# One fused decoder block: x ahead of c in the first stage, Silu of c behind the squares of x

## The chip, the cores and the metric

The kernel runs on one core of one Trainium2 chip. The metric is device time in microseconds of one execution of the whole program; lower is better. The core has five engines with a queue each: PE (TensorE, with its weight loads shown apart as PEld), DVE (VectorE), ACT (ScalarE), POOL (GpSimd) and SP (SyncE, which here only issues DMAs). A queue is worked off in order; an instruction that waits for another engine or for a DMA holds those behind it.

## The reference, cut to what matters

One sequence of 512 tokens, width 1024, one layer, all in float32.

```python
cs  = silu(c)                                   # c: (1, 1024)
mod = cs @ ada_w + ada_b                        # 1024 x 6144
sh_m, sc_m, gt_m, sh_f, sc_f, gt_f = split(mod, 6)
h = rmsnorm(x, norm_mix_g) * (1 + sc_m) + sh_m
q, k, v, g_ret, b_cv, c_cv, u_cv, g_a, g_b = split(h @ w_in)
q, k = rope(q, cos, sin), rope(k, cos, sin) * d**-0.5   # cos, sin of positions * inv_freq
y_a = (silu(g_ret) * head_layernorm(retention(q, k, v))) @ ret_w_out
y_b = (b_cv * causal_conv3(c_cv * u_cv)) @ conv_w_out
x = x + gt_m * ((sigmoid(g_a) * y_a + sigmoid(g_b) * y_b) @ mix_w_out)
# then a SwiGLU feed-forward part with sh_f, sc_f, gt_f, and a last rmsnorm
```

## The kernel before, in words

Features lie on the partitions in tiles of 128 (8 k tiles), tokens along the free axis (512). Every product is made of three matmuls on a high and a low part of each operand, so each weight tile is first cast by ACT (`_h`) and then subtracted by DVE (`_l`).

**First stage (L132 to L436).** SP loads c, then x in four tiles of 512 KB (`x_load`, L333), then the first pair of k tiles of the modulation weights as eight pieces of 256 KB (`ada_load`), then the first weights of c, u, b and k (`w_load`). POOL makes the constants `eps_t`, `ident` and `ones32` and issues the small loads: the rows of ada_b, the two norm gains and conv_w (L150 to L153), positions (`posi`, L155) and inv_freq (`ivf`, L157). ACT takes Silu of c into `cs` (L162) and runs one Sqrt on a constant (`warm`, L165). From L347 on every engine is in strict order, so the code from L398 to L576 is the order of each queue. For each x tile t: `x_squares(t)` (ACT: Square with a sum, then Sqrt), `x_scaled(t)` (DVE: reciprocal and scaling; PE: eight transposes), `x_by_feature(t, h)` (copies out of PSUM on ACT or DVE). `busy(n)` is n matmuls on constants that fill PE's time. `quarters()` makes three small constants from `ident` on DVE (L239). `mod_row` multiplies pieces of ada_w with `cs` on PE into two banks; `ada_sum` adds four other pieces weighted by `cs` on DVE into `acc_m`; `mod_sums` brings these sums into the same banks on PE. The two banks give the gains of the first two k tiles (`a_m`, `s_m`), ACT makes the modulated `Hh` of a k tile with them, and the first products `p_c`, `p_u`, `p_b`, `p_k` start.

**Pairs of k tiles (L545 to L576).** For j = 2, 4, 6 the next pair of modulation weights and of weights is loaded, if there is one, and the products of the pair before run.

**After that (from L577) the order is not written out.** Instructions are given to a scheduler that lays out each engine's queue ahead of time from its own estimate of when operands are ready; what it may estimate, the chip may not find. In this part lie the rotary angles on DVE (`rotary`, L298 and L597 to L601, from `posi` and `ivf` into `fr`), the value projection `p_v`, the tables `ropeC` and `ropeS` (`rope_tables`, L640: eight Sin activations on ACT), `rope` of a k or q tile (L651: four products and a sum on DVE, then a split), and the retention of a head pair. For the first pair the projections come in the order k (heads 0, 1), q (0, 1), gate (0, 1). `scores(u)` (L730) is due some projections later, set by `after(2 + u, ...)`; the first scores tile `st` is three matmuls of the rotated q and k of head 0.

Sin, Silu and Sqrt are activation functions that need a table to be loaded in ACT: an ACT_TABLE_LOAD stands in ACT's queue wherever the next function is not in the table loaded last; Copy, Identity and Square need none of their own.

`tc.issue_after(i)` puts what is issued inside it behind instruction i, on the engine of i.

Of the kernel before, what the change touches and what calls it, by code (L numbers as in the profile page):

```python
# [15 lines left out]
AF = mybir.ActivationFunctionType  # L16
# [3 lines left out]
P = 128  # L20
# [50 lines left out]
def block_kernel(ctx, tc, x, c, positions, ada_w, ada_b, norm_mix_g, w_in, conv_w, ret_w_out,  # L71
# [3 lines left out]
    pe, vec, act, pool, sync = (InTurn(tc, e) for e in (nc.tensor, nc.vector, nc.scalar, nc.gpsimd,  # L75
                                                        nc.sync))
# [13 lines left out]
    def scr(name, dt=F32, shape=None):  # L90
        return tp.tile(shape or [P, S], dt, tag="scr", bufs=12, name=name)
# [4 lines left out]
    def acc(name):  # L96
        return ps.tile([P, S], F32, tag="acc", bufs=4, name=name)
# [33 lines left out]

    HS = S // 2  # L132
    c_sb = cp.tile([P, KT], F32, name="c_sb")
    sync.dma_start(c_sb, c.rearrange("o (p k) -> (o p) k", p=P))
    rows = cp.tile([P, P], F32, name="rows")
    vec.memset(rows, 0.0)
    R_ADA, R_GM, R_GF, R_CW = 0, 48, 56, 64
# [2 lines left out]
    eps_t = cp.tile([P, 1], F32, name="eps_t")  # L140
# [8 lines left out]
    with tc.issue_after(pool.last.ins):  # L149
        small.dma_start(rows[0:48], ada_b.rearrange("o (r p) -> (o r) p", p=P))  # L150
        small.dma_start(rows[48:56], norm_mix_g.rearrange("o (r p) -> (o r) p", p=P))
        small.dma_start(rows[56:64], norm_ffn_g.rearrange("o (r p) -> (o r) p", p=P))
        small.dma_start(rows[64:88], conv_w.rearrange("o t (r p) -> (o t r) p", p=P))  # L153
        for i in range(2):
            small.dma_start(posi[64 * i:64 * i + 64],  # L155
                            positions[0, HS * i:HS * (i + 1)].partition_broadcast(64))
        small.dma_start(ivf, inv_freq.rearrange("(f o) -> f o", o=1))  # L157
# [1 line left out]
    x2 = x[0].rearrange("(t p) (h n) -> t h p n", p=P, n=S)  # L159

    cs = cp.tile([P, KT], F32, name="cs")
    act.activation(cs, c_sb, AF.Silu)  # L162
    warm = cp.tile([P, 1], F32, name="warm")
    with tc.issue_after(act.last.ins):
        act.activation(warm, eps_t, AF.Sqrt)  # L165

    onesr = cp.tile([P, P], F32R, name="onesr")

# [2 lines left out]
    def rows_by_feature(tr):  # L171
        vecs.append(cp.tile([P, P], F32, name="vecs"))
        act.copy(vecs[0], tr[:, 0:P])
# [24 lines left out]
    def ada_load(f, j):  # L198


        s0 = 0 if f == "m" else 3
        cols = slice(j * P, (j + 2) * P)
        ada_raw[f, j] = pieces = []
        for k in range(0, KT, 4):
            raw = wp.tile([P, 4, 2, 2 * P], F32, tag="raw", bufs=3, name=f"ada_{f}{j}_{k}")
            for q, i in ((q, i) for q in range(0, 4, 2) for i in range(2)):
                load_raw.last = sync.dma_start(raw[:, q:q + 2, i],
                                               aw6[:, k + q:k + q + 2, s0 + i, cols])
            pieces += [raw[:, q].rearrange("p s n -> p (s n)") for q in range(4)]
# [16 lines left out]
    def mod_gains(f):  # L226

        r0 = R_ADA + ADA["sc_" + f] // P
        g0 = R_GM if f == "m" else R_GF
        vec.scalar_tensor_tensor(mod["b_" + f], vecs[0][:, r0:r0 + KT], 1.0, vecs[0][:, g0:g0 + KT],  # L230
                                 ALU.add, ALU.mult)
# [7 lines left out]
    def quarters():  # L239
        quart["sum"] = cp.tile([P, 4, QP], F32, name="quart_sum")  # L240
        cols = sp.tile([P, QP], F32, tag="quart", bufs=1, name="quart_cols")
        vec.tensor_reduce(cols, ident.rearrange("p (q c) -> p c q", q=4), axis=AX.X, op=ALU.add)
        vec.tensor_copy(quart["sum"], cols.unsqueeze(1).to_broadcast([P, 4, QP]))
        quart["own"] = cp.tile([P, 4], F32, name="quart_own")
        vec.tensor_reduce(quart["own"], ident.rearrange("p (q c) -> p q c", q=4), axis=AX.X,
                          op=ALU.add)
        quart["f"] = cp.tile([P, 2 * D // QP], F32, name="quart_f")
# [85 lines left out]
    def x_load():  # L333
        for t in range(NT):
            xt = wp.tile([P, 2, S], F32, tag="hi", name=f"x_{t}")
            xs[t] = [xt[:, h] for h in range(2)] + [xt.rearrange("p h n -> p (h n)")]
            load_raw.last = sync.dma_start(xs[t][2], x[0, t * P:(t + 1) * P, :])

    def w_load(k):
        for n in "cubk":  # L340
            cols = P if n == "k" else 2 * P
            w_raw[n, k] = scr(f"w_{n}0_{k}", F32, [P, 2, cols])
            load_raw.last = sync.dma_start(
                w_raw[n, k], wi[k * P:(k + 2) * P, COL[n]:COL[n] + cols].rearrange(
                    "(k p) n -> p k n", p=P))
# [5 lines left out]
    def busy(n):  # L351

        for _ in range(n):
            mm(idle[:, 0:P], lhsT=ident, rhs=ident, start=True, stop=True)
# [8 lines left out]
    def x_squares(t):  # L363
        junk = scr(f"n1_{t}", BF16, [P, D])
        act.activation(junk, xs[t][2], AF.Square, accum_out=ssq[:, t:t + 1])
        act.activation(r4[:, t:t + 1], ssq[:, t:t + 1], AF.Sqrt, scale=1.0 / D, bias=eps_t)

    def x_scaled(t):
        r = r4[:, t:t + 1]
        vec.reciprocal(r, r)  # L370
        vec.tensor_scalar_mul(xs[t][2], xs[t][2], r)
        for h in range(2):
            txs[t, h] = acc(f"tx_{t}{h}").rearrange("p (k n) -> p k n", n=P)
            for k in range(4):
                transpose(txs[t, h][:, k], xs[t][h][:, k * P:(k + 1) * P], ident)
# [7 lines left out]
    def mod_row(j, k, banks, first, cols=range(4)):  # L383


        for i in cols:
            mm(banks[i % 2][:, i * P:(i + 1) * P], lhsT=ada_raw["m", j][k][:, i * P:(i + 1) * P],
               rhs=cs[:, k:k + 1].to_broadcast([P, P]),
               start=first and (i == 0 or i == 1 and banks is apart), stop=False)
# [11 lines left out]
    busy(18)  # L401
    for t in range(2):
        x_squares(t)
    x_scaled(0)
    busy(3)
    x_squares(2)
# [3 lines left out]
    tr = pv("tr_rows")  # L410
    transpose(tr[:, 0:P], rows, ident)
    x_squares(3)
    rows_by_feature(tr)
    x_scaled(2)
    busy(1)
# [5 lines left out]
    x_by_feature(2, 0, act.copy)  # L421
    x_by_feature(2, 1, act.copy)
    mod_gains("m")
    quarters()
    mod_row(0, 1, apart, False)
    a = ada_sum(ada_raw["m", 0][2:6], 4 * P, "m0", None, 2)
    x_by_feature(3, 0, act.copy)
# [15 lines left out]
    hist = []  # L443
    hlast = []

    def w_hi(n, k):
        raws[n, k] = w_raw.pop((n, k))
        wt[n, k] = [slot(f"w_{n}0_{k}_{z}", F32R, raws[n, k].shape) for z in "hl"]
        act.copy(wt[n, k][0], raws[n, k])
# [41 lines left out]
    def some_sums(j, k0, k1):  # L491

        if j < KT:
            sums[j] = ada_sum(ada_raw["m", j][k0:k1], 4 * P, f"m{j}", sums.get(j), k0)

    def products(k):
        ops = []
        parts = (0, 1, 2) if k % 2 else (1, 0, 2)
        for part in parts:
            x = (Hl if part == 2 else Hh)[:, k, :]  # L500
            for n, i in grp:
                w = wt[n, k - k % 2][1 if part == 0 else 0][:, k % 2, :]
                at = k == 0 and part == parts[0], k == KT - 1 and part == 2
                ops.append((gps[n, i], w[:, i * P:(i + 1) * P], x, at, (n, i)))
        if k == KT - 1:
            ops.sort(key=lambda o: grp.index(o[4]))
        if k == 0:
            order = {"c": 0, "u": 1, "b": 2, "k": 3}
            ops = sorted(ops[:14], key=lambda o: order[o[4][0]]) + ops[14:]
        for o, w, x, (first, last), _ in ops:  # L510
            yield mm(o, lhsT=w, rhs=x, start=first, stop=last)

    def run(steps, n=21):
        for _, _ in zip(range(n), steps):
            pass
# [29 lines left out]
    for j in range(2, KT, 2):  # L545
        if j + 2 < KT:
            ada_load("m", j + 2)
            w_load(j + 2)
        steps = products(j - 1)
        run(steps, 14)  # L550
        if j == 2:
            mod_row(j, 7, both, True)
        else:
            some_sums(j, 4, KT)
        for n in "cubk":
            w_hi(n, j)
        if j < KT - 2:
            mod_sums(sums[j], both, j > 2)
            w_lo("c", j)
            mod_cols("m", j, mods.rearrange("p (i n) -> p i n", n=P)[:, :, 0])  # L560
        else:
            mod_quarters(j)
            w_lo("c", j)
            mod_own(j)
        for k in (j, j + 1):
            h_hi(k)
            h_full(k)
        for n in "ubk":
            w_lo(n, j)
        run(steps)  # L570
        some_sums(j + 2, 0, 2)
        h_lo(j)
        run(products(j))
        some_sums(j + 2, 2, 4)
        h_lo(j + 1)
# [684 lines left out]
    for h in range(2):  # L1260
# [16 lines left out]
        for t, cs in tm_gemm(ffn_w_down[0], af, f0, nf, h, groups, 0, "dn", True,  # L1277
# [15 lines left out]
            o = [scr(f"o_{t}{i}") for i in range(2)]  # L1293
# [45 lines left out]
```

## Time and profile before

| | us |
|---|---|
| median of 3 runs | 936.87 (936.76 to 937.35) |
| the profiled execution, its own time | 937.46 |
| span of the profile | 935.7 |
| PE busy | 927.3 |
| DVE busy | 623.9 |
| ACT busy | 358.9 |

The profile is of one execution. Rows of the timeline give the start, the duration, the engine, the line, the operation with out<-in by the program's names (numbers left out), the shape and the count; in square brackets stands the idle time just before, and what ended it. The chain of waits is followed back from the last instruction, each step to what released it. A matmul's duration is longer than the distance to the next one, since matmuls overlap; a 128x512 matmul follows the one before it every 0.227 us (rows of p_q at 93.92 and 94.14). The granted TensorE clock was 0.999 in the whole execution.

### The profile page before, as it was taken

The page shows a single profiled execution, that of the slowest core. Times are in us where ns is not written, and L with a number is a line of the kernel's source. Part 1 is how long each engine was busy: PE and PEld are TensorE (multiplying, and loading weights), DVE is VectorE, ACT ScalarE, POOL GpSimd, SP SyncE. Part 2 cuts the span into 40 slices and gives each one's busy share as a digit, 9 for nine tenths or more (in the row PEclk, how much of TensorE's full clock was granted, in tenths as well). Part 3 has the DMA queues.
Part 4 walks back from the last instruction along what each step waited for, and adds up shares of the span by engine and source line. Part 5 has one row for each costly group of instructions (what it writes and reads, how often), then busy time and mean ns, then how long its engine had stood idle before and what let it go on. Part 6 is the DMA issues. An engine that isn't in the chain of part 4 may idle for free.

```text
span 935.7 us, 11163 instructions
## 1 busy us (share of the span) xinstructions
PE 927.3 (99%) x4299; PEld 774.9 (83%) x4299; DVE 623.9 (67%) x1001; ACT 358.9 (38%) x531; POOL 37.6 (4%) x72
## 2 busy tenths in 40 slices
PE   8999999999999999999999999999999999999997
PEld 8888888888888888888888888988888888888886
DVE  5999784797868566654674457667665545566575
ACT  7534432544444333222233235423433223443324
POOL 2000000000001000000000000000011000001000
PEclk9999999999999999999999999999999999999999
DMA  9943423322463537765553552445578672368912
GB/s 324 338 156 107 136 73 102 102 72 98 153 218 102 180 103 244 215 203 191 170 190 113 180 181 89 136 152 190 198 248 269 225 255 72 102 168 233 334 63 90
DMA packets 119909, 158.49 MB, mean 169 GB/s; under 512 B 5476, under 2 KB 94864, under 8 KB 118704
## 3 DMA queue, kind: packets, MB, share of 16 engines
q1 hardware_dynamic: 114672, 139.61, 45.3%
q0 software_dynamic: 5040, 18.04, 6.0%
q8 instruction: 33, 0.54, 0.2%
q14 instruction: 20, 0.16, 0.1%
q10 hardware_dynamic: 144, 0.13, 0.0%
HBM read 139.91 MB, written 17.85 MB: 169 GB/s over the span
## 4 chain that ended last, share of the span: by engine, by line
PE 96%; DVE 1%; ACT 1%; DMA 1%; SPq 0%; issue 0%; DVEq 0%
PE p_fu L64 13%; PE p_fg L64 12%; PE dn_t L64 5%; PE p_g L64 5%; PE p_yb L64 5%; PE p_gb L64 5%; PE p_q L64 5%; PE p_v L64 5%; PE p_ya L64 5%; PE p_ga L64 5%; PE p_k L64 4%; PE dn_b L64 4%; PE p_b L64 4%; PE p_u L64 4%; PE p_c L64 3%; PE mix L64 3%
## 5 line engine op out<-in xcount | busy, mean ns | idle before, releaser
L64 PE MATMUL p_fu<-Gh,w_fu_l 128*128 128x512 f32 x160 | 62.4, 390 | 0.0
L64 PE MATMUL p_fu<-Gh,w_fu_h 128*128 128x512 f32 x160 | 62.3, 389 | 0.0
L64 PE MATMUL p_fu<-Gl,w_fu_h 128*128 128x512 f32 x160 | 62.2, 389 | 0.0
L64 PE MATMUL p_fg<-Gh,w_fg_l 128*128 128x512 f32 x160 | 62.2, 389 | 0.0
L64 PE MATMUL p_fg<-Gl,w_fg_h 128*128 128x512 f32 x160 | 62.2, 389 | 0.0
L64 PE MATMUL p_fg<-Gh,w_fg_h 128*128 128x512 f32 x160 | 62.2, 389 | 0.0
L64 DVE TENSOR_TENSOR w_bl<-w_bl 128x512 f32<-128x512 f32 x36 | 24.8, 688 | 26.7 <-DMA w_bl<-in_ffn_w_down_dram 26.4
L64 ACT CAST w_fu_h<-w_fu 128x1024 fp32r<-128x1024 f32 x20 | 21.0, 1054 | 56.2 <-PE p_fu L64 33.3
L64 DVE TENSOR_TENSOR w_fg_l<-w_fg,w_fg_h 128x1024 fp32r<-128x1024 f32 x20 | 24.3, 1219 | 25.3 <-ACT w_fg_h L64 25.2
L64 DVE TENSOR_TENSOR w_b_l<-w_b,w_b_h 128x1024 fp32r<-128x1024 f32 (+1 forms) x21 | 24.0, 1146 | 22.2 <-ACT w_b_h L64 22.1
L64 ACT ACTIVATE fg<-p_fg 128x512 f32<-128x512 f32 x22 | 13.1, 598 | 62.5 <-PE p_fg L64 62.5
L64 PEld LDWEIGHTS p_fu<-Gh,w_fu_h 128*128 128x128 f32 x160 | 30.0, 188 | 6.3
L64 PEld LDWEIGHTS p_fg<-Gh,w_fg_h 128*128 128x128 f32 x160 | 30.0, 188 | 6.3
L64 PEld LDWEIGHTS p_fu<-Gh,w_fu_l 128*128 128x128 f32 x160 | 30.0, 188 | 6.2
L64 PEld LDWEIGHTS p_fg<-Gh,w_fg_l 128*128 128x128 f32 x160 | 30.0, 188 | 6.2
L64 PEld LDWEIGHTS p_fg<-Gl,w_fg_h 128*128 128x128 f32 x160 | 30.0, 188 | 6.2
L64 PEld LDWEIGHTS p_fu<-Gl,w_fu_h 128*128 128x128 f32 x160 | 30.0, 188 | 6.2
L64 DVE TENSOR_TENSOR fg<-p_fu,fg 128x512 f32<-128x512 f32 x22 | 15.2, 690 | 27.8 <-PE p_fu L64 27.8
L64 DVE TENSOR_TENSOR w_t_l<-w_t,w_t_h 128x1024 fp32r<-128x1024 f32 (+1 forms) x20 | 22.2, 1115 | 13.9 <-ACT w_t_h L64 13.8
L64 ACT CAST w_t_h<-w_t 128x1024 fp32r<-128x1024 f32 (+1 forms) x20 | 19.4, 968 | 25.5 <-PE dn_t L64 12.7
L64 ACT CAST w_b_h<-w_b 128x1024 fp32r<-128x1024 f32 (+1 forms) x21 | 20.8, 989 | 20.4 <-issue 7.9
L64 ACT CAST sh<-sm 128x512 fp32r<-128x512 f32 (+3 forms) x32 | 14.7, 460 | 35.3 <-DVE sm L64 35.2
(438 smaller groups left out, 2713.3 us busy)
## 6 DMA issues: line engine op xcount, KB each, us to landing
w_fg<-in_ffn_w_gate_dram SPq DMA_DIRECT2D x11, 1024.0 KB, 5.5
w_fu<-in_ffn_w_up_dram SPq DMA_DIRECT2D x11, 1024.0 KB, 5.8
w_bl<-in_ffn_w_down_dram SPq DMA_DIRECT2D x18, 512.0 KB, 4.7
blocks<-w_bl POOLq DMA_DIRECT2D x9, 1024.0 KB, 5.2
ada_m<-in_ada_w_dram SPq DMA_DIRECT2D x32, 256.0 KB, 5.4
ada_f<-in_ada_w_dram SPq DMA_DIRECT2D x32, 256.0 KB, 4.2
w_t<-blocks SPq DMA_DIRECT2D x8, 1024.0 KB, 5.6
w_b<-in_ffn_w_down_dram SPq DMA_DIRECT2D x6, 1024.0 KB, 5.0
```

Of the source, the lines that this page charges most:

```text
L64: self.last = op(*args, **kw)
```

## The change

SP loads x ahead of c. Silu of c, which stood ahead of everything on ACT, moves behind the Square and Sqrt of the last x tile; the Sqrt on a constant stays and now stands first. `quarters()` moves from behind `mod_gains` to behind the squares of the first two tiles. The loads of `posi` and `ivf` are put into a function that is called where j = 6, inside an `issue_after` on the last `h_hi` activation.

```diff
     c_sb = cp.tile([P, KT], F32, name="c_sb")
-    sync.dma_start(c_sb, c.rearrange("o (p k) -> (o p) k", p=P))
...
         small.dma_start(rows[64:88], conv_w.rearrange("o t (r p) -> (o t r) p", p=P))
+
+    def rotary_loads():
         for i in range(2):
             small.dma_start(posi[64 * i:64 * i + 64],
                             positions[0, HS * i:HS * (i + 1)].partition_broadcast(64))
...
     cs = cp.tile([P, KT], F32, name="cs")
-    act.activation(cs, c_sb, AF.Silu)
     warm = cp.tile([P, 1], F32, name="warm")
-    with tc.issue_after(act.last.ins):
-        act.activation(warm, eps_t, AF.Sqrt)
+    act.activation(warm, eps_t, AF.Sqrt)
...
             load_raw.last = sync.dma_start(xs[t][2], x[0, t * P:(t + 1) * P, :])
+        sync.dma_start(c_sb, c.rearrange("o (p k) -> (o p) k", p=P))
...
     for t in range(2):
         x_squares(t)
+    quarters()
     x_scaled(0)
...
     x_squares(3)
+    act.activation(cs, c_sb, AF.Silu)
     rows_by_feature(tr)
...
     mod_gains("m")
-    quarters()
     mod_row(0, 1, apart, False)
...
             w_load(j + 2)
+        else:
+            with tc.issue_after(hist[-1].ins):
+                rotary_loads()
         steps = products(j - 1)
```

The queues that come out of it are shown at three places. First ACT in the first stage; `n1_3` is the square of the last x tile, `r4` its Sqrt. Before, at the queue's start and behind the last square:

```order
L64 ACT_TABLE_LOAD
L64 ACTIVATE cs_97<-c_sb_75 128x8
L64 ACT_TABLE_LOAD
L64 ACTIVATE warm_99<-eps_t_79 128x1
L62 ACTIVATE n1_0_169,ssq_121<-x_0_125 128x1024
```

```order
L62 COPY xT_0_117<-tx_00_177 128x2x128
L62 COPY xT_2_118<-tx_00_177 128x2x128
L62 ACTIVATE n1_3_211,ssq_121<-x_3_131 128x1024
L62 ACTIVATE r4_122<-ssq_121,eps_t_79 128x1
L62 COPY vecs_214<-tr_rows_209 128x128
```

Of the changed kernel, behind the last square:

```order
L62 ACTIVATE n1_3_214,ssq_116<-x_3_126 128x1024
L62 ACTIVATE r4_117<-ssq_116,eps_t_78 128x1
L62 ACT_TABLE_LOAD
L62 ACTIVATE cs_93<-c_sb_75 128x8
L62 COPY vecs_218<-tr_rows_212 128x128
```

The second table load and `cs` moved from the queue's start to between the last Sqrt and the copy of `vecs`. Two later table loads, ahead of the first Sin and ahead of the first Silu of a gate, are no longer in the queue.

Second PE, where the projection of q of head 0 (`p_q00`) ends and that of head 1 (`p_q01`) begins; `st0_0` is the first scores tile. Before:

```order
L64 MATMUL p_q00_941<-Hh_115,w_q00_l_939 128x512
L64 MATMUL p_q00_941<-Hl_116,w_q00_h_937 128x512
L64 MATMUL p_q00_941<-Hh_115,w_q00_h_937 128x512
L64 MATMUL p_q01_980<-Hh_115,w_q01_l_978 128x512
L64 MATMUL p_q01_980<-Hl_116,w_q01_h_976 128x512
```

Of the changed kernel:

```order
L64 MATMUL p_q00_941<-Hl_111,w_q00_h_937 128x512
L64 MATMUL p_q00_941<-Hh_110,w_q00_h_937 128x512
L64 MATMUL st0_0_1085<-q00_h_972,k00_l_891 128x512
L64 MATMUL p_q01_980<-Hh_110,w_q01_l_978 128x512
L64 MATMUL p_q01_980<-Hl_111,w_q01_h_976 128x512
```

One of the three matmuls of `st0_0` moved ahead by 72 matmuls, from behind the second gate projection to between the two q projections; the other two stay where they were.

Third DVE at the same place in the program: `k00`, `k01`, `q00` are rotated tiles (`_a`, `_b` their two halves of the sum), `v03` the last value tile. Before, and of the changed kernel in two pieces:

```order
L64 TENSOR_TENSOR w_q00_l_939<-w_q0_935,w_q00_h_937 128x1024
L64 TENSOR_TENSOR v03_c_870<-p_v03_842,v03_m_867 128x512
L64 TENSOR_TENSOR w_q01_l_978<-w_q0_935,w_q01_h_976 128x1024
L64 TENSOR_TENSOR v03_l_873<-v03_c_870,v03_h_872 128x512
L64 TENSOR_TENSOR w_g00_l_1023<-w_g0_1019,w_g00_h_1021 128x1024
L64 TENSOR_TENSOR k00_a_884<-p_k00_123,ropeC_738 128x512
```

```order
L64 TENSOR_TENSOR w_q00_l_939<-w_q0_935,w_q00_h_937 128x1024
L64 TENSOR_TENSOR v03_c_870<-p_v03_842,v03_m_867 128x512
L64 TENSOR_TENSOR k00_a_884<-p_k00_118,ropeC_738 128x512
L64 TENSOR_TENSOR k00_b_885<-p_k00_118,ropeS_739 64x512
L64 TENSOR_TENSOR v03_l_873<-v03_c_870,v03_h_872 128x512
```

```order
L64 TENSOR_TENSOR q00_a_966<-p_q00_941,ropeC_738 128x512
L64 TENSOR_TENSOR q00_b_967<-p_q00_941,ropeS_739 64x512 x2
L64 TENSOR_TENSOR k01_l_932<-k01_a_925,k01_h_931 128x512
L64 TENSOR_TENSOR q00_a_966<-q00_a_966,q00_b_967 128x512
L64 TENSOR_TENSOR w_q01_l_978<-w_q0_935,w_q01_h_976 128x1024
L64 TENSOR_TENSOR q00_l_973<-q00_a_966,q00_h_972 128x512
```

The low part of the weights of q of head 1 (`w_q01_l`) and that of the first gate moved from ahead of the rotations to behind the rotated q of head 0.

In POOL's queue the loads of `posi` and `ivf` stand where they stood, right behind that of conv_w, and no wait stands with them: the last `h_hi` is an instruction of ACT, and the loads are issued by POOL. SP's queue has x first, then c, then the same loads as before.

## Prediction

> **What bounds the kernel now.** I read the page first, then what PE waits for, then the chain of waits. The page has a span of 935.7 us, and PE is busy in nearly all of it; of PE's waits behind 17.6 us only one is long enough to be listed:
>
> ```profile
> PE 927.3 (99%) x4299; PEld 774.9 (83%) x4299; DVE 623.9 (67%) x1001; ACT 358.9 (38%) x531; POOL 37.6 (4%) x72
> ...
> PE mods L62 <- DVE acc_m L62: 0.3, 1, 0.3
> ```
>
> So from about 17 us to the end PE runs one matmul behind the other. Whatever delays PE by a microsecond at one place delays the end by one, and nothing later can absorb it; work saved on another engine is worth nothing unless PE waits for it. Ahead of 17 us the chain of waits goes through other engines (start, length, what):
>
> ```profile
> 2.60 8.23 DMA x<-in_x_dram
> 10.85 1.16 ACT n L62 x2
> ...
> 12.04 0.30 ACT r L62
> ...
> 12.56 0.75 DVE x L62
> ...
> 13.39 0.30 DVE quart_cols L62
> ...
> 13.86 0.28 DVE quart_own L62
> 14.14 0.41 DVE acc_m L62
> ...
> 16.93 0.50 DVE acc_m L62
> ...
> 17.47 0.89 PE mods L62 x4
> ...
> 19.69 1.15 PE p_c L62 x4
> ```
>
> The last x tile lands at 10.85; its square, its scaling, `quarters` and the sums `acc_m` follow, and at 17.47 PE gets the sums. These are the steps that the change rearranges. There are two parts to cost: this first stage, and the place near 94 us where the queues came out in another order.
>
> **The first stage.** The timeline of it:
>
> ```profile
> 0.74 0.39 SPq L64 DMA_DIRECT2D c_sb<-in_c_dram  x1
> 1.19 1.84 SPq L62 DMA_DIRECT2D x<-in_x_dram  x4
> ...
> 2.59 1.28 ACT L64 ACT_TABLE_LOAD   x1
> ...
> 3.88 0.20 ACT L64 ACTIVATE warm<-eps_t 128x1 f32<-128x1 f32 x1
> ...
> 12.33 0.30 PEld L62 LDWEIGHTS mods<-cs,ada_m 128*128 128x128 f32 x2
> 13.43 0.86 PEld L62 LDWEIGHTS tx<-ident,x 128*128 128x128 f32 x8
> 14.48 0.30 PEld L62 LDWEIGHTS mods<-cs,ada_m 128*128 128x128 f32 x2
> 15.38 1.20 PEld L62 LDWEIGHTS idle<-ident 128*128 128x128 f32 x10
> 16.49 0.53 PEld L62 LDWEIGHTS mods<-cs,ada_m 128*128 128x128 f32 x4
> 16.74 0.62 ACT L62 CAST w_c_h<-w_c 128x512 fp32r<-128x512 f32 x1 [1.41 <-DMA w_c<-in_w_in_dram]
> ```
>
> x first: its loads begin at 0.74 instead of 1.19, 0.45 us earlier. How much earlier the last tile lands the trace can't show; it is at least 0 (if the bytes set it), and perhaps 0.9 (twice the head start, if the small packets of c held x up as well). I take 0.45, so 10.40: nothing else in front of x changes.
>
> Silu of c behind the squares: on ACT now stand, behind the last x tile, the square (1.16), the Sqrt (0.30), the table load (1.28) and `cs` (0.21, which I take from the 0.20 of `warm`). So `cs` is there 3.0 us behind the landing, at 13.4 instead of before 3. Who waits: PE's first `mods<-cs,ada_m`, which ran at 12.33 and now runs at 13.45, and behind it, in order, all of PE's first stage. By the starts in the rows: eight of these matmuls 0.90 (as from 14.48 to 15.38), the transposes and a fill 1.05 (13.43 to 14.48), eight more 0.90, the fill 1.11 (15.38 to 16.49), four more 0.45. That is 4.4, so the sums' matmuls can start at 17.85. Before, PE came there early and waited until 17.47. It is 0.4 late, and `p_c` with it.
>
> VectorE's constants first: `quarters` leaves the chain (13.39 to 14.14, 0.75 us). But `acc_m` needs `cs`, and the gains ahead of it on DVE need `vecs`, which ACT copies behind `cs`; so `acc_m` starts after 13.4, at my estimate at 13.8, instead of at 14.14, and what it gains (0.3) is hidden by PE's 17.85. The rest of ACT's stage starts at 13.4 instead of 12.3, 1.1 late; ACT stood idle for 1.41 in front of the cast at 16.74, which covers it. So the stage costs +0.4 with x 0.45 earlier, +0.85 with x no earlier, and -0.05 with x 0.9 earlier.
>
> The Trainium skill (ScalarE: Activation LUTs, What ACT_TABLE_LOAD costs) counts a drain of about 1.38 us with each 1.28 us table load. By that the stage would cost some 1.4 us more; in the rows above `warm` starts at 3.88, right where the load from 2.59 ends, so here the trace doesn't show it and the sum goes without.
>
> Positions: they are not moved. `posi` and `ivf` stand in POOL's queue where they stood, without a wait, so this edit costs and brings nothing.
>
> **The place near 94 us.** One matmul of the first scores tile now stands between the two q projections. Its operand is the high part of the rotated q of head 0, which is made of the very projection that ends just ahead of it. PE works in order, so the 24 matmuls of the second q projection stand behind this wait. Before, the rows at this place were:
>
> ```profile
> 93.92 0.39 PE L64 MATMUL p_q<-Hh,w_q_h 128*128 128x512 f32 x1
> 94.14 0.39 PE L64 MATMUL p_q<-Hh,w_q_l 128*128 128x512 f32 x1
> ...
> 110.46 0.39 PE L64 MATMUL st<-q_h,k_l 128*128 128x512 f32 x1
> ```
>
> ```profile
> 84.93 0.44 DVE L62 TENSOR_SCALAR fr<-fr 128x512 f32<-128x512 f32 x1
> ...
> 87.06 0.71 DVE L64 TENSOR_TENSOR v_c<-p_v,v_m 128x512 f32<-128x512 f32 x1
> 87.66 1.24 DVE L64 TENSOR_TENSOR w_q_l<-w_q,w_q_h 128x1024 fp32r<-128x1024 f32 x1
> 88.80 0.71 DVE L64 TENSOR_TENSOR v_l<-v_c,v_h 128x512 fp32r<-128x512 f32 x1
> ...
> 90.53 0.71 DVE L64 TENSOR_TENSOR k_a<-p_k,ropeC 128x512 f32<-128x512 f32 x1
> ...
> 97.34 1.39 DVE L64 TENSOR_TENSOR q_b<-p_q,ropeS 64x512 f32<-64x512 f32 x2
> ...
> 99.37 0.69 DVE L64 TENSOR_TENSOR q_a<-q_a,q_b 128x512 f32<-128x512 f32 x1
> ```
>
> ```profile
> 85.10 1.28 ACT L64 ACT_TABLE_LOAD   x1
> 86.39 0.42 ACT L64 ACTIVATE ropeC<-fr 64x256 f32<-64x256 f32 x1
> ...
> 89.58 0.40 ACT L64 ACTIVATE ropeS<-fr 64x256 f32<-64x256 f32 x1
> ...
> 100.79 0.61 ACT L64 CAST q_h<-q_a 128x512 fp32r<-128x512 f32 x1
> ```
>
> Before, `q_h` was there at 101.4, and the scores came at 110.46, with 9 us in hand. Now I work out when it is there, first without the 0.4 of the first stage, which moves all of it alike. The table load at 85.10 is gone, so the Sines start when `fr` is ready, at 85.4. Before, they took 86.39 to 89.98 with one cast (about 0.65 from start to start, its own 0.62 and a gap) among them; now eight in a row take 2.95, and the last `ropeC` (0.4 ahead of the end) is there at 88.05. DVE has ended `v_c` at 87.8 and starts the rotations at 88.1. In before the same instructions, from `k_a` at 90.53 to the end of the sum `q_a` at 100.06, took 9.53; now one `v_l` (0.6, the step from 88.80 to 89.40 in a back-to-back queue) stands among them. So `q_a` is there at 98.2, its cast (0.61) at 98.9, and PE's scores matmul starts near 98.9. The second q projection also needs `w_q_l`, which was made at 87.66 and now stands behind `q_a` in DVE's queue: 98.2 + 1.24 = 99.4. So the projection starts at 99.45 instead of 94.14: 5.3 us of PE, in which the one scores matmul (0.23) is done that is missing later. Net 5.1.
>
> The bounds: had DVE nothing else to do, the chain from the projection's end (93.92 + 0.39 = 94.3) is a product 0.71, two more 1.39, a sum 0.69, then `w_q_l` 1.24, so 98.4, and the net cost 4.0. If DVE reaches the rotations later than I think by the length of another split (1.24), it is 6.3. It isn't below 4.0 unless PE passes a waiting matmul.
>
> Behind this place DVE and ACT have 5 us more in hand than before, and no other matmul has moved, so nothing else gets late. The two table loads that are dropped from ACT bring nothing: PE didn't wait for ACT.
>
> **Sum.** 0.4 + 5.1 = 5.5. The profiled execution took 937.46 of its own, 0.6 above the median of the runs, and would take 943.0; the median of 936.87 becomes 942.4.
>
> **The rivals.** *PE falls back to a slower pace in the gap.* PE would stand idle from 94.3 to 98.9, 4.6 us. Such a gap doesn't occur in the trace behind the first matmuls. But at its start the same matmul on constants was slower (mean ns, first until 4.6 us, then from 5.6 us; below them the pace, five in a row against ten):
>
> ```profile
> L62 PE MATMUL idle<-ident 128*128 128x128 f32 x12 | 2.8, 421 | 0.0
> ...
> L62 PE MATMUL idle<-ident 128*128 128x128 f32 x18 | 2.2, 275 | 0.0
> ```
>
> ```profile
> 2.07 1.27 PE L62 MATMUL idle<-ident 128*128 128x128 f32 x5
> ...
> 15.48 1.28 PE L62 MATMUL idle<-ident 128*128 128x128 f32 x10
> ```
>
> From start to start that is (1.27 - 0.42)/4 = 0.21 us against (1.28 - 0.275)/9 = 0.11. PE began at 1.49 and was slow until between 4.6 and 5.6, so 3.1 to 4.1 us at half pace, a loss of 1.6 to 2.0. If the gap puts PE back there, the second q projection pays 1.8 more: 944.2. For it: the gap is longer than the warming up took. Against: no row shows how long an idle time it takes. I give it 0.32. The Trainium skill (TensorE: Matmul & The Clock Gate, The HAM clock gate) says that the rate halves after at least one idle window of about 3.4 us, and that the windows run freely; by that a gap of 4.6 us does it in some executions and not in others, and the trace agrees as far as its slow start goes.
>
> *PE isn't held there*, because matmuls that are ready go past the one that waits, or the operand is there in time. Then only the first stage counts: 936.87 + 0.4 = 937.3, and, if x lands over 0.85 us earlier, slightly below 936.87. This is the case that is not slower. Against it: at 17.47 the wait for `acc_m` held PE with more matmuls that don't read it queued behind (L434, the second round), and `q_h` would have to be there by 94.3, where the projection it is made of has only just ended. I give it 0.10.
>
> *A gain of the first stage decides alone*: no hold, and DVE's chain sets the stage instead of PE; x 0.45 and `quarters` 0.75 earlier would be 1.2, so 935.7. It takes a `cs` that doesn't wait for its table, against the row at 2.59. 0.03.
>
> **How the numbers follow.** The forecast has 0.55, the slow pace 0.32, no hold 0.10, the gain 0.03. The likeliest is 942.4. Its own range is 936.87 + 4.0 + 0 to 936.87 + 6.3 + 0.85, so 940.9 to 944.0; with the slow pace the upper end reaches 942.4 + 2.0 + some 0.8 of the hold's upper bound, 945.2. I take 941.0 to 945.2. A measurement of this kernel can tell about 0.2% (1.9 us) from no change. The first two cases are slower by more than that; a hold of half the size would still be. Slower 0.87; no hold is the same, 0.11 with its edges; faster 0.02, since even 1.2 us of gain lies within the bound.
>
> **What would show it.** In the profile of the changed kernel: the last Sqrt of the stage, a table load of 1.28 and `cs` in a row on ACT, `mods<-cs` near 13.4 and `p_c` 0.4 later than 19.69; among PE's waits one of about 4.6 us in front of `st`, put down to ACT `q_h`, near 95 to 99, and a shorter one in front of `p_q` for DVE `w_q_l`; behind it the same matmuls 5.5 later. If the matmuls behind the gap follow every 0.43 instead of 0.227, it is the slow pace. Wrong would be: no wait in front of `st`, `st` behind `p_g`, or a stage that ends earlier than 17.47.

## The result, and the profile after

The changed kernel took 944.23 us (median of 5 runs, 943.21 to 944.86), the kernel before 937.03 beside it (936.76 to 937.69): ratio 1.0075, interval 1.0064 to 1.0085. So it is slower by 7.2 us, above the 942.4 of the forecast and inside its range. The profiled execution took 944.23 of its own, with a span of 942.4 us; against the 937.46 and 935.7 of the profile before that is 6.77 and 6.7 more.

Engine busy times of the changed kernel, and all that PE waits for:

```profile
PE 929.6 (99%) x4299; PEld 776.3 (82%) x4299; DVE 624.5 (66%) x1001; ACT 356.0 (38%) x529; POOL 37.6 (4%) x72
```

```profile
PE st L64 <- ACT q_h L64: 4.6, 1, 4.6
PE idle L64 <- POOL ident masks.py:199: 1.5, 1, 1.5
PE mods L62 <- ACT cs L62: 0.9, 1, 0.9
```

PE does 2.3 us more of "work" with the same number of instructions, and has a wait of 4.6 us in front of `st` that wasn't there. The chain of waits in the first stage (start, length, what) now goes through ACT, without a break from the landing of the first x tile to `cs`, and then through PE alone:

```profile
0.74 3.72 DMA x<-in_x_dram
...
4.48 1.16 ACT n L62 x2
...
9.22 1.06 ACT n L62 x2
...
10.62 1.28 ACT L62
...
11.91 0.22 ACT cs L62
...
12.18 0.49 PE mods L62 x2
...
18.82 1.15 PE p_c L62 x4
```

The last square starts at 9.12 instead of 10.85 (the chain's 9.22 leaves out its first tenth, in which a copy still ran), and PE's first `p_c` comes at 18.82 in this chain, against 19.69. The first stage is 0.87 us shorter in this execution than in the profiled one of before.

PE at the place near 94 us (timeline: start, length, engine, line, operation; in brackets the idle time before and what ended it):

```profile
93.08 0.39 PE L64 MATMUL p_q<-Hh,w_q_h 128*128 128x512 f32 x1
98.09 0.80 PE L64 MATMUL st<-q_h,k_l 128*128 128x512 f32 x1 [4.62 <-ACT q_h L64]
98.68 0.75 PE L64 MATMUL p_q<-Hh,w_q_l 128*128 128x512 f32 x1
99.23 0.63 PE L64 MATMUL p_q<-Hl,w_q_h 128*128 128x512 f32 x1
99.66 0.63 PE L64 MATMUL p_q<-Hh,w_q_h 128*128 128x512 f32 x1
...
103.86 0.39 PE L64 MATMUL p_q<-Hh,w_q_l 128*128 128x512 f32 x1
104.09 0.39 PE L64 MATMUL p_q<-Hl,w_q_h 128*128 128x512 f32 x1
...
106.60 0.39 PE L64 MATMUL p_g<-Hh,w_g_l 128*128 128x512 f32 x1
```

The second q projection starts at 98.68 instead of 94.14, and its first matmuls follow each other every 0.43 us (99.23, 99.66) instead of 0.227, up to 103.86. The windows view (a stretch; its length; busy time of PE, PEld, DVE, ACT, POOL; the granted clock; share of the DMA engines; GB/s) shows why:

```profile
96.00:97.00 1.00, 0.00 (x0) 0.00 (x0) 0.97 (x3) 0.00 (x0) 0.00 (x0) 0.97 0.00 0
97.00:98.00 1.00, 0.00 (x0) 0.00 (x0) 1.00 (x2) 0.58 (x1) 0.00 (x0) 0.50 0.00 0
...
103.00:104.00 1.00, 1.00 (x4) 0.79 (x3) 0.00 (x0) 0.00 (x0) 0.00 (x0) 0.62 1.06 387
```

The clock is 0.50 from 96.94 (a mean of 0.97 over the microsecond is 0.06 us at half) to 103.76 (0.62 is 0.76 us at half). That is 6.82 us at half pace, 1.15 of them while PE still waited.

So the profile adds up, place by place: first stage -0.87; start of the second q projection 98.68 - 94.14, which with the 0.87 added back is +5.41; half pace (106.60 - 98.68) - (99.58 - 94.14) = +2.48; one scores matmul less later, -0.23. The sum is 6.79, against 6.77.

### The profile page after: what moved, and what is told of

Its sections match the earlier page's. It is cut to its first block, busy times and chain, and to the rows that moved or that the text cites. A ratio compares the mean times of both kernels' runs of the same rounds, so it can differ in the third digit from the quotient of the medians.

```text
span 942.4 us, 11161 instructions
## 1 busy us (share of the span) xinstructions
PE 929.6 (99%) x4299; PEld 776.3 (82%) x4299; DVE 624.5 (66%) x1001; ACT 356.0 (38%) x529; POOL 37.6 (4%) x72
## 4 chain that ended last, share of the span: by engine, by line
PE 91%; DVE 5%; ACT 2%; issue 1%; DMA 0%; DVEq 0%
PE p_fu L64 13%; PE p_fg L64 12%; PE dn_t L64 5%; PE p_g L64 5%; PE p_yb L64 5%; PE p_gb L64 5%; PE p_ya L64 5%; PE p_ga L64 5%; PE p_q L64 4%; PE dn_b L64 4%; PE p_k L64 3%; PE p_b L64 3%; PE p_u L64 3%; PE p_c L64 3%; PE mix L64 3%; PE p_v L64 2%
```

## The experiments

Unless said otherwise an edit is one to the changed kernel; the kernel before took 936.9 to 937.2 us beside all of them.

**Is the scores matmul the whole of it?** It was held behind the last matmul issued before it in the program, which puts PE's queue back as it was before; DVE's stays as changed.

```diff
             st = aux(f"st{p}_{u}")
-            mm3(st[:, 0:n], ...
+            with tc.issue_after(pe.last.ins):
+                mm3(st[:, 0:n], ...
```

> The changed kernel, with the scores matmuls kept behind the matmul that was written ahead of them, so that PE's queue is the one of before. Theory A (the loss is the one scores matmul ahead of the second q projection, its wait of 4.6 us and the slower pace behind it): both go, the first stage's gain of 0.9 us stays, the first p_c matmul stays at 18.8, and the time is about 936.1, 0.9 below before. Rival B (the loss comes from what else moved there, the low parts of the weights behind the rotations on DVE and the dropped table loads on ACT): PE still waits near 93 us, now for DVE's w_q_l or w_g_l, and the time stays at 941 or above.

Measured: 944.58 us (943.93 to 945.0), ratio 1.0081 (1.0067 to 1.0094). No gain at all. PE now waits for something else, and for as long (PE, and the DVE row that ends the wait):

```profile
99.35 0.76 PE L64 MATMUL p_q<-Hh,w_q_l 128*128 128x512 f32 x1 [5.22 <-DVE w_q_l L64]
```

```profile
97.38 0.69 DVE L64 TENSOR_TENSOR q_a<-q_a,q_b 128x512 f32<-128x512 f32 x1
97.98 1.22 DVE L64 TENSOR_TENSOR w_q_l<-w_q,w_q_h 128x1024 fp32r<-128x1024 f32 x1
```

The low part of the weights of the second q projection stands in DVE's queue behind the rotated q of head 0. That alone holds PE for 5.2 us. The theory that the one scores matmul carries the loss fell; there are two locks side by side, and opening one leaves the other.

**Which edit brings it?** The kernel before, with Silu of c moved behind the squares and nothing else.

```diff
-    act.activation(cs, c_sb, AF.Silu)
     warm = cp.tile([P, 1], F32, name="warm")
-    with tc.issue_after(act.last.ins):
-        act.activation(warm, eps_t, AF.Sqrt)
+    act.activation(warm, eps_t, AF.Sqrt)
...
     x_squares(3)
+    act.activation(cs, c_sb, AF.Silu)
     rows_by_feature(tr)
```

> Before, with Silu of c behind the squares as the one edit (c still loaded first, constants and positions where they were). Theory A: this edit alone drops two later table loads, turns the queue over and brings the wait and the slow pace (5.2 + 2.5), and without the earlier x the first stage is 0.9 us late: about 945.5. Rival D (the early x or the constants are needed for the loss): no wait in front of st, and about 937.9.

Measured: 943.7 us (943.57 to 944.51), ratio 1.0073 (1.0059 to 1.0087). PE's wait for `q_h` is there, 4.63 us:

```profile
98.63 0.80 PE L64 MATMUL st<-q_h,k_l 128*128 128x512 f32 x1 [4.63 <-ACT q_h L64]
```

So the move of Silu by itself brings the loss; the order of x and c, the constants and the positions aren't needed for it. The 945.5 that was expected is 1.8 too high: in the profiled execution `p_c` comes at 19.34, so the first stage isn't late, and the clock is at half for 3.4 us and not for 6.8.

**Is it Silu's place in the first stage, or what it leaves in ACT's tables?** Two kernels turn this around. In the first, everything of the change stays, and one Sqrt of one column is added near 46 us, where ACT is idle for 5 us. Its table is then the last one loaded, so the first Sin and the first Silu of a gate each need a load again, as before.

```diff
         for n in "cubk":
             w_hi(n, j)
+        if j == KT - 2:
+            warm2 = cp.tile([P, 1], F32, name="warm2")
+            act.activation(warm2, eps_t, AF.Sqrt)
```

> The changed kernel with one more Sqrt of one column on ScalarE near 45 us, in its 5.4 us of idle time. All of the change to the first stage stays; only ScalarE's table has to be loaded again ahead of the first Sin and the first gate Silu, and with that the instruction queues of TensorE, VectorE and ScalarE behind 20 us are those of the kernel before. Theory A (the loss comes from the queues near 94 us, and these turn on ScalarE's tables): 936.0 to 937.0 us, no wait of TensorE over 1 us behind 20 us, its first p_c at 18.8 to 19.6 us, granted clock 1.00 from 94 to 104 us. Rival B (the late Silu itself, or c behind x, brings a loss of its own that the 7 us hide): 938 us or more.

Measured: 937.16 us (11 runs, 936.73 to 937.72), ratio 1.0002 (0.9993 to 1.001). The whole loss is gone, though the time is 0.2 above the range of theory A. ACT, with the load ahead of the first Sin back, and PE at the place, without a wait:

```profile
84.43 1.28 ACT L64 ACT_TABLE_LOAD   x1
85.72 0.42 ACT L64 ACTIVATE ropeC<-fr 64x256 f32<-64x256 f32 x1
```

```profile
93.93 0.39 PE L64 MATMUL p_q<-Hh,w_q_h 128*128 128x512 f32 x1
94.15 0.39 PE L64 MATMUL p_q<-Hh,w_q_l 128*128 128x512 f32 x1
```

The second kernel is the one before, its first stage untouched, with one Silu of one column at the same place; the two later loads then fall away.

```diff
         for n in "cubk":
             w_hi(n, j)
+        if j == KT - 2:
+            warm2 = cp.tile([P, 1], F32, name="warm2")
+            act.activation(warm2, eps_t, AF.Silu)
```

> The kernel before, first stage untouched, with one Silu of one column on ScalarE near 45 us. The queues of TensorE and VectorE near 94 us are then those of the changed kernel. Theory A: the scores matmul waits about 4.6 us, the second q projection starts 5.1 to 5.4 us later than before, and the slow pace adds 1.8 to 2.5 us: 943.8 to 944.8 us, first p_c at 19.6 us as before; without the slow pace 942.0. Rival C (the stage's shift in time makes the wait, not the queues): 937 us.

Measured: 944.3 us (944.2 to 944.91), ratio 1.0079 (1.0067 to 1.0092), with the same wait of PE:

```profile
PE st L64 <- ACT q_h L64: 4.6, 1, 4.6
```

One activation of a single column, far from both the first stage and the place near 94 us, makes the whole loss in the one kernel and takes it away in the other. What changed is which table ACT holds when the first Sin comes, and with it two table loads of 1.28 us. The scheduler lays out the queues from its estimate; with the loads gone it puts the rotations earlier on DVE and `w_q_l` behind them. That the loads decide the queues is shown; by which step of the estimate is not.

**Is the slower pace behind the wait due to the idle time?** Matmuls were put into the gap, 20 of them in one kernel and 8 in another. They write the accumulator of the second q projection, which its own first matmul clears.

```diff
...
+            pt = acc(f"p_{name}{i}")
+            if name == "q0" and i == 1:
+                for _ in range(20):
+                    with tc.issue_after(pe.last.ins):
+                        mm(pt, lhsT=wh[:, 0, :], rhs=Ah[:, 0, :], start=True, stop=True)
+                filled.append(pe.last)
...
-            mm3(st[:, 0:n], ...
+            with tc.issue_after(filled[0].ins):
+                mm3(st[:, 0:n], ...
```

> The changed kernel with 20 matmuls of 512 columns put between the first q projection and the scores matmul; they write the accumulator of the second q projection, which starts over behind them, so the output is the same. They fill 4.5 of the 4.6 us for which PE waits. Theory A (the slow pace comes of the idle time): the second q projection follows at 0.227 us, 2.5 us are won, and the time is about 941.7. Rival C (the pace falls for another reason, such as the loads that start at 99 us or the small first matmul): it is slow again, and the time is 944.2.

Measured with 20: 942.31 us (941.96 to 942.47), ratio 1.0056 (1.0043 to 1.0069). The second q projection starts at 99.23, no earlier than in the other kernels, but at full pace:

```profile
99.23 0.50 PE L64 MATMUL p_q<-Hh,w_q_l 128*128 128x512 f32 x1
...
104.78 0.39 PE L64 MATMUL p_g<-Hh,w_g_l 128*128 128x512 f32 x1
```

The first gate projection follows 5.55 us later, as before the change (5.44) and unlike the changed kernel (7.92). With more work on PE the kernel takes 1.9 us less than the changed one, though not the 941.7 of theory A; in this execution `p_c` came at 19.45, and theory A had counted with 18.8.

> The same with 8 matmuls, which leaves PE idle for about 2.8 us. The scheduler brings one more scores matmul (384 columns) forward, which takes about 0.17 in the wait and saves it later. If 2.8 us of idle time are too short to bring the slow pace (PE was slow for 3.7 us at the start of the profile): about 941.5. If they are long enough: about 944.

Measured with 8: 943.49 us, but spread from 941.72 to 944.69, nearly six times as wide as with 20; ratio 1.0068 (1.0056 to 1.0081). PE's gap and the clock in its profiled execution:

```profile
98.92 0.68 PE L64 MATMUL st<-q_h,k_l 128*128 128x512 f32 x2 [2.85 <-ACT q_h L64]
```

```profile
99.00:100.00 1.00, 1.00 (x5) 0.73 (x6) 1.00 (x3) 0.00 (x0) 0.00 (x0) 0.99 0.00 0
100.00:101.00 1.00, 1.00 (x4) 0.81 (x3) 1.00 (x1) 0.00 (x0) 0.00 (x0) 0.50 0.29 72
...
103.00:104.00 1.00, 1.00 (x5) 0.82 (x4) 0.36 (x1) 0.00 (x0) 0.00 (x0) 0.81 1.09 384
```

After 2.85 us of idle time the clock still fell, and only at 99.98, when PE had been at work again for a microsecond. It came back at 103.38.

**Opening the other lock.** The low part of the second q weights is made ahead of the rotary step of the first q head. The scheduler then puts the scores matmul back behind the gate by itself.

```diff
...
+            elif i == 0:
+                both_w = [split(raw[:, :, h * P:(h + 1) * P], [P, KT, P], f"w_{name}{h}")
+                          for h in range(2)]
+                early.append(vec.last)
...
+        if name == "q00":
+            with tc.issue_after(early[0].ins):
+                vec.tensor_tensor(a, pt, ropeC, ALU.mult)
```

> The changed kernel with the low part of the second q weights made ahead of the rotary step of the first q head on VectorE; the scores matmul stands behind the gate projection again. By the trace of the changed kernel the low part then runs at 94.0 to 95.2 us, where TensorE is free at 93.1: a wait of about 2.1 us. Theory A (the loss is this wait, and the slow pace needs a longer one): 936.9 - 0.9 to 0 + 2.1 = 938.1 to 939.0 us, granted clock 1.00 throughout. Rival D (the slow pace comes with a wait of 2 us too): 939.9 to 941.5, with matmuls 0.43 us apart behind the wait.

Measured: 940.63 us (7 runs), ratio 1.0033 (1.0022 to 1.0045). Five runs lie at 940.56 to 940.83, two at 938.70 and 938.89, and none between. The profiled one is of the first group:

```profile
95.88 0.47 PE L64 MATMUL p_q<-Hh,w_q_l 128*128 128x512 f32 x1 [1.88 <-DVE w_q_l L64]
```

```profile
95.00:96.00 1.00, 0.12 (x1) 0.15 (x2) 1.00 (x2) 0.65 (x2) 0.00 (x0) 1.00 0.00 0
96.00:97.00 1.00, 1.00 (x4) 0.75 (x5) 0.99 (x3) 0.00 (x0) 0.00 (x0) 0.66 0.16 19
...
99.00:100.00 1.00, 1.00 (x4) 0.81 (x3) 1.00 (x2) 0.00 (x0) 0.00 (x0) 0.63 1.08 386
```

The lock costs what it holds, 95.88 - 94.14 = 1.7 us: 937.0 + 1.7 is the lower group. The upper group pays 1.9 more, the half pace, which here came with 1.88 us of idle time. Theory A held for the hold and failed for the pace (rival D). No run of the lower group was profiled, so that its clock stayed at 1.00 is inferred. Besides its time the mean clock of each run on record agrees with it: 0.998 and 0.999 in the lower group, 0.996 or 0.997 in the upper one, where 3.41 us at half take 0.0018 off the mean.

In the next kernel this low part comes earlier still, ahead of the rotary step of the second k head, so that it is there before PE wants it.

```diff
...
+        raw = load_raw(wi, 0, KT, COL["q"], 2 * P, "w_q0")
+        for h in range(2):
+            early.append(split(raw[:, :, h * P:(h + 1) * P], [P, KT, P], f"w_q0{h}"))
+        early.append(vec.last)
...
+        if name == "k01":
+            with tc.issue_after(early[2].ins):
+                vec.tensor_tensor(a, pt, ropeC, ALU.mult)
```

> The changed kernel, two table loads less than before, with the low part of the second q weights ahead of the rotary step of the second k head on VectorE; it then ends near 91.2 us, before TensorE needs it at 93.1. The scores matmul comes behind the second q projection by itself. Theory A: no wait at the second q projection; TensorE waits 0 to 1.2 us for the cast or for the first gate's low part near 99 us: 936.2 to 938.1 us, at full pace unless the wait is over 1.5 us. Rival F (something else in the changed queues costs): over 939 us.

Measured: 937.53 us (11 runs, 937.27 to 938.2), ratio 1.0005 (0.9996 to 1.0014). `w_q_l` is made at 90.75, and all that PE still waits for there is

```profile
PE st L64 <- ACT q_h L64: 0.5, 1, 0.5
```

This opens both locks without a table load more, and nothing else in the changed queues costs anything that can be measured.

**PE's lock alone.** The kernel with the Sqrt at 46 us, and two matmuls ahead of the second q projection, of which the first reads the cast of the first q head; DVE makes `w_q_l` early, as before.

```diff
...
+            if name == "q0" and i == 1:
+                mm(pt, lhsT=wh[:, 0, :], rhs=rotated["q00"], start=True, stop=True)
+                with tc.issue_after(pe.last.ins):
+                    mm(pt, lhsT=wl[:, 0, :], rhs=Ah[:, 0, :], start=True, stop=True)
```

> The changed kernel with the Sqrt at 45 us (queues of the kernel before, the second q weights' low part early on VectorE), and one matmul more that reads the cast of the first q head, ahead of the second q projection: TensorE's lock alone, without VectorE's. (Its product is overwritten by the next matmul.) Theory A (a matmul that waits for the cast holds all behind it, whatever VectorE did before): the cast ends near 100.7 us in this order of VectorE, TensorE free at 93.1 to 93.9: a wait of 6.5 to 6.9 us; with two matmuls more and a slow pace of 1.6 to 3.2 us: 944.5 to 947 us. Rival E (only VectorE's late low part costs; the scores matmul waited because of it): 937.6 us.

Measured: 946.82 us (945.76 to 947.21), ratio 1.0101 (1.0087 to 1.0115), with this wait:

```profile
PE p_q L64 <- ACT q_h L64: 6.5, 1, 6.5
```

So a matmul that waits for this cast holds everything behind it, also with the weights long ready. Each of the two locks is enough by itself.

**A mix of both first stages.** c through ACT's own DMA queue, Silu and both table loads at the front of ACT, x first in SP's queue, the constants early.

```diff
+    nc.scalar.dma_start(c_sb, c.rearrange("o (p k) -> (o p) k", p=P))
...
+    act.activation(cs, c_sb, AF.Silu)
     warm = cp.tile([P, 1], F32, name="warm")
-    act.activation(warm, eps_t, AF.Sqrt)
+    with tc.issue_after(act.last.ins):
+        act.activation(warm, eps_t, AF.Sqrt)
...
-        sync.dma_start(c_sb, c.rearrange("o (p k) -> (o p) k", p=P))
...
-    act.activation(cs, c_sb, AF.Silu)
```

> A mix of both kernels: x stands first in the first queue, c goes through ScalarE's own DMA queue at its start, Silu of c and the Sqrt table come first on ScalarE as before, and VectorE makes its constants first as changed. Queues behind 20 us as before. Theory A: c's small packets run beside x; x's last tile lands near 9.0 us if the order in the queue decides (first p_c at 18.8 us, 936.0), near 10.8 if the packets share the transfer engines all the same (19.6 us, 936.9). Rival B (the first square waits for c and the two table loads, 2 us later than in the changed kernel): first p_c at 20 us or later, 937.3 or more.

Measured: 937.16 us (11 runs, 936.96 to 937.33), ratio 1.0001 (0.9993 to 1.001), first `p_c` at 19.40. c lands 4.1 us after its issue, and the first square stands behind the second table load until 6.45, 2 us later than in the changed kernel, as rival B has it; `p_c` is no later than before for that. `p_c` lies between theory A's two times, and the kernel's time is that of the kernel before.

**Is the gain of the first stage real?** Both kernels once more, unchanged, each in one profiled execution.

> The kernel before, unchanged, in a second profiled execution. Theory A (the first profile of before caught a late landing of the last x tile): the last square starts at 9.7 us, not 10.85, and the first p_c at 19.3 to 19.5 us. Rival G (the first stage of before always ends at 19.64): square at 10.8, p_c at 19.6 to 19.7 us.

> The changed kernel, unchanged, in a second profiled execution. Theory A (the landing of x varies by a microsecond from execution to execution): first p_c anywhere from 18.8 to 19.6 us; the scores matmul waits 4.6 us again; the clock is 0.50 for 3.4 or 6.8 us. Rival G (the change makes the first stage 0.87 us shorter each time): p_c at 18.7 to 18.9 us.

Measured: 937.57 us with `p_c` at 19.85 for the one before, 943.27 us with `p_c` at 19.05 for the changed one. The last square of x in the two, and in the kernel before with the Silu at 46 us, whose first stage is that of the one before:

```profile
11.06 1.06 ACT L62 ACTIVATE n<-x 128x1024 bf16<-128x1024 f32 x1 [0.54 <-DMA x<-in_x_dram]
```

```profile
9.54 1.07 ACT L62 ACTIVATE n<-x 128x1024 bf16<-128x1024 f32 x1
```

```profile
9.73 1.06 ACT L62 ACTIVATE n<-x 128x1024 bf16<-128x1024 f32 x1
```

The 9.7 that theory A expected of the kernel before did not come: its second profile has the last square even later than its first. Only the third row, of another kernel with that stage, has it. With the same first stage the last square starts at 10.85, 11.06 or 9.73, and `p_c` at 19.64, 19.85 or 19.49. In the nine executions that have the changed stage the last square starts between 9.12 and 10.14 and `p_c` lies between 18.77 and 19.65, 19.2 in the mean; a gain of 0.87 each time (rival G) is out. A gain of some 0.4 in the profiles, then, and in the time none that can be told from zero: the kernel with the Sqrt at 46 us has the changed stage and the queues of before, and its ratio is 1.0002 (0.9993 to 1.001).

## Why the prediction came out as it did

**What bounds the kernel: right.** The changes of PE's schedule add up to the difference of the two executions within 0.02 us.

**The first stage: wrong, by its first term.** "I take 0.45, so 10.40" is the step that failed. The last x tile no longer ended the wait for the last square at all: the square started at 9.12, when ACT was free. The rest of the working holds from there: `cs` is there 3.0 us behind the square's start, as forecast, PE's first `mods` comes at 12.18, and the 4.4 us of PE's work up to the sums are 4.45 (its weight loads at 12.17 and 16.62). PE got the sums at 16.73, and "a stage that ends earlier than 17.47" was one of the prediction's own signs of being wrong. So the sign turned, -0.87 for +0.4 in the profiled executions. The landing had been read from one execution as if it were the kernel's own: with c ahead of x the last square starts at 9.73, 9.74 (the kernel before with Silu late), 10.85 and 11.06, 10.3 in the mean, and with the changed stage at 9.7 in the mean, 0.6 earlier. So few profiles don't separate what of this the order of the loads brings from what chance does.

**The hold: right in size.** Forecast 5.3 and net 5.1, measured 5.4 and 5.2. (85.4 + 2.95 - 0.4 is 87.95 for the last `ropeC`, not the prediction's 88.05; no term of the sum changes by it.) Each step of the chain was found, 0.87 earlier for the first stage: the Sines 84.52 to 87.45 (2.93 us, 2.95 forecast), the first rotation 87.17 (88.1), the rotated q at 97.39 (98.2), `st` at 98.09 (98.9). The rows of DVE and ACT that set the end of it:

```profile
87.17 0.69 DVE L64 TENSOR_TENSOR k_a<-p_k,ropeC 128x512 f32<-128x512 f32 x1 [0.28 <-ACT ropeC L64]
...
96.70 0.69 DVE L64 TENSOR_TENSOR q_a<-q_a,q_b 128x512 f32<-128x512 f32 x1
97.30 1.22 DVE L64 TENSOR_TENSOR w_q_l<-w_q,w_q_h 128x1024 fp32r<-128x1024 f32 x1
```

```profile
97.42 0.62 ACT L64 CAST q_h<-q_a 128x512 fp32r<-128x512 f32 x1 [2.30 <-DVE q_a L64]
```

What was off is the weight given to the two causes. The text led with the scores matmul and took `w_q_l` as the last half microsecond of the hold; the rival "PE isn't held there", with matmuls going past the one that waits, overlooked that they would have met `w_q_l` at once. The experiments show two locks of about 5 us that overlap. The shorter wait for `w_q_l` that the prediction listed among its signs isn't in the profile: `w_q_l` ended at 98.52, while the scores matmul ran, and the projection came at 98.68.

**The pace: the step on which the likeliest case was chosen, and it failed.** "Against: no row shows how long an idle time it takes" left the rival at 0.32. Half the clock came behind the gap in each profiled execution that had one of 1.9 us or more, and filling the gap with matmuls took it away. The price was 1.8 by the start of the trace (the windows view has 1.00 there, but only because the trace's records of the clock begin with the full one, at 5.28 us in the kernel before, which fits the slow matmuls until then); measured 2.48 in the first profile and, in the second one of the same kernel, (105.70 - 98.94) - 5.44 = 1.3. The first had two stretches at half pace, the second had one, begun 0.2 us before PE went on. The five runs of the changed kernel agree with this: 943.21 and 943.50 us with a mean clock of 0.996 and 0.997, and 944.23 to 944.86 with 0.995. That the rival's time, 944.2, is the measured one is luck in part: in the profiled execution the first stage was 1.3 us better than forecast and the pace 0.7 worse than the rival's, which cancel by half, and by the rival's terms that execution would have taken 937.46 + 0.4 + 5.1 + 1.8 = 944.8. The forecast's own range ended at 944.0; the time is inside the stated one because that had been widened for the slow pace.

**The table loads.** "The two table loads that are dropped from ACT bring nothing" was right of PE's waits for ACT and missed their part: they are why the queues came out in another order. The prediction read the new order off and asked for its price, not for its cause.

**Positions: right.** `posi` is issued by POOL at 3.80 as its queue has it, with the rows ahead and no wait.

The Trainium skill (ScalarE: Activation LUTs, What ACT_TABLE_LOAD costs) counts a drain of about 1.38 us with a load; the trace differs again: the Sqrt ahead of the load ends at 10.60, the load at 10.62 takes 1.28, and `cs` starts at 11.91.

## What to carry to other kernels

When a scheduler lays out the queues, compare every engine's queue over the whole program after an edit, not only near it: here one activation function moved in the first 10 us changed which table loads stand at 85 us, and through them the order at 94. If PE waits for an operand, look for the second operand behind it before the first is blamed. And count a gap of PE of about 2 us or more with its length and, in many executions, 1.3 to 2.5 us behind it; where the gap can't be closed, filling it with matmuls keeps the pace.

## What the hardware showed that wasn't expected

The half pace comes in stretches of one length, which the windows view gives to some 0.02 us: 3.40 us (99.98 to 103.38) after the gap of 2.85, 3.42 (96.32 to 99.74) after that of 1.88, and 6.82, two of them, in the changed kernel's first profile and behind the wait of 6.5. The kept traces hold the clock's own records, which are finer: 3.413 us for one stretch and 6.827 for two. They also show that stretches follow each other without a break. From the first record of the full clock to the fall are 92.160 us in the changed kernel, 95.573 in the kernel with 8 matmuls and 88.747 in that with the gap of 1.88, which is 27, 28 and 26 times 3.413. Where the borders lie differs from execution to execution: the first full clock is recorded between 4.40 and 7.58 us.

In these traces a stretch falls into half pace by what PE did in the 3.41 us ahead of it. PE was busy there for none of it in the changed kernel, 1.06 us (31%) with the gap of 2.85, and 1.5 us (45%) with the gap of 1.88, where it ran until 94.00 and again from 95.88. The kernel before with the Silu has these rows of PE and of its windows:

```profile
98.78 0.50 PE L64 MATMUL st<-q_h,k_l 128*128 128x512 f32 x1 [4.64 <-ACT q_h L64]
```

```profile
98.00:99.00 1.00, 0.22 (x1) 0.19 (x1) 1.00 (x2) 0.62 (x1) 0.00 (x0) 1.00 0.00 0
99.00:100.00 1.00, 0.93 (x3) 0.57 (x3) 1.00 (x3) 0.00 (x0) 0.00 (x0) 0.66 0.00 0
```

PE stopped at 94.14, and its clock fell at 99.32. The stretch from 92.49 to 95.91 had PE busy for 1.66 us (48%), and the clock stayed at 1.00 behind it. The end of the program narrows this further. First the kernel with the scores held, then the one with Silu alone, two stretches each:

```profile
935.17:938.59 3.42, 1.54 (x13) 1.33 (x12) 2.82 (x10) 2.76 (x10) 0.00 (x0) 1.00 0.76 293
938.59:942.00 3.41, 0.00 (x0) 0.00 (x0) 0.52 (x2) 0.28 (x1) 0.00 (x0) 0.50 0.46 167
```

```profile
934.55:937.96 3.41, 1.59 (x14) 1.39 (x12) 2.81 (x10) 2.75 (x10) 0.00 (x0) 1.00 0.75 289
937.96:941.37 3.41, 0.00 (x0) 0.00 (x0) 0.58 (x2) 0.34 (x1) 0.00 (x0) 1.00 0.47 172
```

Behind 1.54 us of work (45%) the clock fell, behind 1.59 (47%) it stayed. So the border lies between 45% and 47% in these traces, each a single execution, by a busy time whose ends are modelled. The way back asks for more: the stretch at half in which PE worked 66% of the time (the changed kernel, from 98.09) was followed by another at half, the one with 87% (the scores held, from 99.35) was not. With such a border a gap of about 2 us counts when it falls within one stretch and not when it is cut by the end of one, which agrees with the two groups of runs 1.9 us apart; that the lower group's gaps were cut so is not shown.

The Trainium skill (TensorE: Matmul & The Clock Gate, The HAM clock gate) states a window of 3413 ns that runs freely; the trace agrees with the length, and with the borders at whole multiples of it. The same page of the Trainium skill (HAM oscillation — how this bites in real kernels) gives as a rule no idle gaps of PE above about 3.4 us; here 1.88 us was enough, by the clock in the profiled run and by their times in four others of seven, and the measurement decides.
